# First block of a hybrid decoder layer: meta tokens loaded last and transposed in the second half, two scales earlier, weight units split in quarters

## The chip, the cores and the metric

The kernel runs on one core of one Trainium2 chip. The metric is device time in microseconds (us), as the median of several runs of the same program; smaller is better. The five engines of the core each work through a queue of their own in order: TensorE (PE; its weight loads are listed as PEld), VectorE (DVE), ScalarE (ACT), GpSimd (POOL) and SyncE (SP), which here issues the DMAs. They wait for each other through semaphores.

## The reference

One decoder layer over 16 learned meta tokens and 512 tokens of width 2048, in float32. Cut to what matters here:

```python
meta = jnp.broadcast_to(meta_tokens[None], (bsz, N_META, D_MODEL))
h_stream = jnp.concatenate([meta, x], axis=1)        # (1, 528, 2048)
hn = rmsnorm(h_stream, norm_w[l])                    # per token: x * rsqrt(mean(x*x) + eps) * w
proj = hn @ w_in[l]                                  # 2048 -> 12320 columns
c_val, c_gate, c_silu, z, xbc, dt_raw = jnp.split(proj, splits, axis=-1)
...                                                  # Conformer branch, Mamba-2 SSD branch
h_stream = h_stream + y @ w_out[l]
out = rmsnorm(h_stream, final_norm_w)[:, N_META:]
```

## The kernel before

Nearly all of the time goes to the input projection, in channel tiles of 128 columns, and to the output projection. Each product is made of three TensorE passes over operands split in a high and a low part (`hi*hi`, `hi*lo`, `lo*hi`). Both projections need the normalized tokens transposed: for each of the 16 blocks of 128 channels a tile `hnh[k]` and a tile `hnl[k]` of 128 channels x 528 tokens, the first 16 columns for the meta tokens.

The change is in the **first block**, which makes these tiles and, since tokens and weights arrive one after the other, also does the first `z` (gate) columns and the `dt` columns. It stands in a section where the order of every engine's work is written by hand, so each engine executes what the code lists, in that order:

- SP loads the meta tokens (`xm`), the token tiles `xt[0]` and `xt[1]` in halves of 512 KB, five weight units `zraw`, `xt[2]`, three more units, `xt[3]`, small parameters, and the first three weight units of the main stream (`wraw`, 512 KB each). A second copy of the meta tokens goes by GpSimd's queue, since all 128 rows of `xm` must hold finite numbers.
- TensorE first turns filler transposes (`busy`, 72 of them, constant `WARM`) until token data is there.
- The row scale of each token tile (`rs`) comes from sums of squares on ScalarE and VectorE, a square root on ScalarE (`rstd_of`) and three small VectorE steps. VectorE scales the token tiles in place (`scale`). For the meta tokens it makes `rdiag`, a diagonal matrix, so that a product of `xm` with `rdiag` scales and transposes at once.
- **First half**: for k = 0 to 15 `tok_a(k)` puts the meta product and the transposes of `xt[0]` and `xt[1]` into one PSUM bank `hta`; `fill` has ScalarE write `hnh` from it (272 columns) and queues VectorE's step for `hnl`, which `lows` hands out. Three steps later (`LAG`) `z_step` multiplies block k with its weights, six products (L357 to L359).
- **Second half**: the same for `xt[2]` and `xt[3]` (`tok_b`, bank `htb`, 256 columns), with `dt_step` for the meta tokens and `dt` columns from k = 8 on. `z_done(1)` and `z_done(2)` (k = 3 and 4) apply Silu on ScalarE, which loads another function table first. `split_unit` (k = 5, 8, 11) converts a weight unit of 1024 columns on ScalarE and subtracts on VectorE.

Four PSUM banks (`sm`) serve `hta` and `htb` in turn, so that four blocks can be on their way. A tile's readers and writers are kept apart by semaphores for the tile as a whole.

## Time and profile before

| | us |
|---|---|
| runs | 1576.78, 1576.80, 1577.02 |
| median | 1576.8 |
| the profiled execution | 1577.11 |
| its span, first to last instruction | 1575.4 |
| TensorE busy | 1565.0 (99%) |
| VectorE busy | 1070.5 (68%) |
| ScalarE busy | 536.5 (34%) |
| GpSimd busy | 51.1 (3%) |

The profiled execution is one run of the same program; its span lies 1.7 us below its time. Engine names, lines and tiles are those of the program; a row of the timeline gives the start, the duration, the engine, the line, the operation, what is written from what, how many instructions were merged (x), and in brackets how long the engine stood idle and what ended that. Matmuls overlap in the pipeline, so the time a matmul takes from a stream is the distance from its start to the next start, not its duration.

### The profile page before, as it was taken

To read this page: it belongs to the slowest core of one execution; us is meant where nothing else is said; L and a number is where in the kernel's file an instruction comes from. 1 tells how busy PE (TensorE), PEld (TensorE's weight loads), DVE (VectorE), ACT (ScalarE), POOL (GpSimd) and SP (SyncE) were. 2 spreads that over 40 slices of the span, in tenths; PEclk is the share of its full clock that TensorE was granted. 3 is DMA by queue.
4 is the path that set the end of the run, shared out by engine and by line. 5 is a ranking of instruction groups with operands and counts; after the bars stand their busy time and mean duration, and the time that the engine had idled before them with its cause. 6 is when DMAs were issued, how large, how long until landed. Compare 5 with 4: busy or idle time off the path is not lost.

```text
span 1575.4 us, 25091 instructions
## 1 busy us (share of the span) xinstructions
PE 1565.0 (99%) x10340; PEld 1437.8 (91%) x10340; DVE 1070.5 (68%) x1840; ACT 536.5 (34%) x839; POOL 51.1 (3%) x138
## 2 busy tenths in 40 slices
PE   9999999999999999999999999999999999999997
PEld 9999998999998999999899999988888888888886
DVE  7658989577998685999866899986625422232323
ACT  6443332333323333333423333324525222122313
POOL 1000000000000000000000000000000001010100
PEclk9999999999999999999999999999999999999999
DMA  8343333333333333433333333236333522222323
GB/s 225 81 114 97 102 94 100 104 92 88 110 90 102 95 106 82 108 94 99 103 97 92 99 103 92 72 108 198 94 94 108 186 95 99 99 96 94 121 94 120
DMA packets 213239, 167.27 MB, mean 106 GB/s; under 512 B 8452, under 2 KB 177252, under 8 KB 212836
## 3 DMA queue, kind: packets, MB, share of 16 engines
q1 hardware_dynamic: 212948, 165.27, 35.8%
q8 instruction: 81, 1.33, 0.4%
q14 instruction: 34, 0.28, 0.1%
q10 hardware_dynamic: 144, 0.26, 0.0%
q0 software_dynamic: 32, 0.13, 0.0%
HBM read 157.19 MB, written 8.45 MB: 105 GB/s over the span
## 4 chain that ended last, share of the span: by engine, by line
PE 99%; ACT 0%; DVE 0%; issue 0%; POOL 0%; DVEq 0%; POOLq 0%
PE o L978 8%; PE o L977 8%; PE o L979 7%; PE gt L322 4%; PE vl L322 4%; PE gt L321 4%; PE vl L321 4%; PE gt L323 4%; PE vl L323 4%; PE cs L323 4%; PE cs L321 4%; PE cs L322 4%; PE z L619 3%; PE z L618 3%; PE z L617 3%; PE xa L322 2%
## 5 line engine op out<-in xcount | busy, mean ns | idle before, releaser
L70 DVE TENSOR_TENSOR wlo<-wraw,whi 128x1024 fp32r<-128x1024 f32 x252 | 314.9, 1250 | 369.7 <-ACT whi L69 364.9
L69 ACT CAST whi<-wraw 128x1024 fp32r<-128x1024 f32 x252 | 264.4, 1049 | 738.9 <-PE o L979 246.6
L596 DVE SCALAR_TENSOR_TENSOR cv<-ub,cw,cv 128x512 f32<-128x512 f32 x480 | 359.0, 754 | 8.2
L978 PE MATMUL o<-wlo,yh 128*128 128x512 f32 x512 | 201.3, 393 | 0.0
L979 PE MATMUL o<-whi,yl 128*128 128x512 f32 x512 | 201.2, 393 | 0.0
L977 PE MATMUL o<-whi,yh 128*128 128x512 f32 x512 | 201.0, 393 | 0.0
L321 PE MATMUL vl<-hnh,whi 128*128 128x256 f32 (+1 forms) x512 | 147.0, 287 | 0.0
L321 PE MATMUL gt<-hnh,whi 128*128 128x256 f32 (+1 forms) x512 | 146.4, 286 | 0.0
L322 PE MATMUL gt<-hnl,whi 128*128 128x256 f32 (+1 forms) x512 | 146.2, 286 | 0.0
L322 PE MATMUL vl<-hnl,whi 128*128 128x256 f32 (+1 forms) x512 | 146.1, 285 | 0.0
L323 PE MATMUL gt<-hnh,wlo 128*128 128x256 f32 (+1 forms) x512 | 145.3, 284 | 0.0
L323 PE MATMUL vl<-hnh,wlo 128*128 128x256 f32 (+1 forms) x512 | 145.2, 284 | 0.0
L977 PEld LDWEIGHTS o<-whi,yh 128*128 128x128 f32 x512 | 96.2, 188 | 22.0
L978 PEld LDWEIGHTS o<-wlo,yh 128*128 128x128 f32 x512 | 96.1, 188 | 22.1
L979 PEld LDWEIGHTS o<-whi,yl 128*128 128x128 f32 x512 | 96.1, 188 | 22.1
L321 PE MATMUL cs<-hnh,whi 128*128 128x512 f32 x256 | 101.7, 397 | 0.0
L323 PE MATMUL cs<-hnh,wlo 128*128 128x512 f32 x256 | 101.0, 394 | 0.0
L322 PE MATMUL cs<-hnl,whi 128*128 128x512 f32 x256 | 100.5, 392 | 0.0
L321 PEld LDWEIGHTS gt<-hnh,whi 128*128 128x128 f32 x512 | 96.6, 189 | 0.0
L321 PEld LDWEIGHTS vl<-hnh,whi 128*128 128x128 f32 x512 | 96.5, 189 | 0.0
L323 PEld LDWEIGHTS gt<-hnh,wlo 128*128 128x128 f32 x512 | 96.5, 188 | 0.0
L323 PEld LDWEIGHTS vl<-hnh,wlo 128*128 128x128 f32 x512 | 96.5, 188 | 0.0
(891 smaller groups left out, 3455.2 us busy)
## 6 DMA issues: line engine op xcount, KB each, us to landing
wraw<-in_w_in_dram SPq DMA_DIRECT2D x188, 512.0 KB, 4.0
wraw<-in_w_out_dram SPq DMA_DIRECT2D x64, 512.0 KB, 3.6
abc<-acum_d SPq DMA_DIRECT2D x32, 256.0 KB, 3.5
yssd_d<-yout SPq DMA_DIRECT2D x16, 256.0 KB, 2.6
ysr<-yssd_d SPq DMA_DIRECT2D x16, 256.0 KB, 5.2
out_dram<-h SPq DMA_DIRECT2D x14, 256.0 KB, 2.4
xt<-in_x_dram SPq DMA_DIRECT2D x6, 512.0 KB, 7.0
h<-in_x_dram SPq DMA_DIRECT2D x3, 1024.0 KB, 7.6
```

Source lines behind the costliest of these rows:

```text
L69: nc.scalar.copy(hi[:, c], raw[:, c])
L70: engine.tensor_sub(lo[:, c], raw[:, c], hi[:, c].bitcast(F32))
L321: T.matmul(o, hi, hnh[kk][:, c0:c0 + n], start=first, stop=False)
L322: T.matmul(o, hi, hnl[kk][:, c0:c0 + n], start=False, stop=False)
L323: T.matmul(o, lo, hnh[kk][:, c0:c0 + n], start=False, stop=last)
L596: V.scalar_tensor_tensor(o, ub[:, k:k + SEQ], cw[:, KT * k + j:KT * k + j + 1], o, op0=ALU.mult, op1=ALU.add)
L617: T.matmul(o, hnh[kk][:, c0:c0 + P], hi[:, k], start=first, stop=False)
L618: T.matmul(o, hnh[kk][:, c0:c0 + P], lo[:, k], start=False, stop=False)
L619: T.matmul(o, hnl[kk][:, c0:c0 + P], hi[:, k], start=False, stop=last)
L977: T.matmul(banks[t], yhi[k][:, ts], hi[:, q], start=first, stop=False)
L978: T.matmul(banks[t], yhi[k][:, ts], lo[:, q], start=False, stop=False)
L979: T.matmul(banks[t], ylo[k][:, ts], hi[:, q], start=False, stop=last)
```

## The change

`WARM` falls from 72 to 52. The meta tokens are loaded by one DMA, after `xt[3]`; VectorE clears all of `xm` at the start; the second copy and GpSimd's two memsets of `xm` are gone. `rdiag`, the meta products (L303) and the early reduction for the meta row are gone; `tok_a` fills 256 columns. The square of the meta row moves to ScalarE at the end of the first half, its root to k = 0 of the second half, and ScalarE scales `xm` in four parts of 512 columns at k = 0 to 3. At k = 4 to 11 `tok_m` transposes two blocks of `xm` per step, four blocks to a bank `htm`, each followed by a `fill` of 16 columns. The scales of `xt[2]` and `xt[3]`, columns 512 to 1023, are handed out one token block earlier. The first three weight units are converted in quarters of 256 columns at k = 2 to 13; the loads of units 3 to 5 move accordingly. Two more filler transposes stand in the middle (14 for 12).

```diff
--- before.py
+++ after.py
@@ -37,7 +37,7 @@
 NCH = 5
 GZ = {1: 2, 3: 2, 5: 2, 7: 1}
 EARLY = 100000
-WARM = 72
+WARM = 52
 LAG = 3
 PVB = 2
 
@@ -62,12 +62,19 @@
 
     def split(self, i, raw, k, engine, parts=1):
         nc, n = self.nc, raw.shape[1]
-        hi = self.pool.tile([P, 1024], F32R, tag="whi", bufs=3, name=f"whi{i}")[:, :n]
-        lo = self.pool.tile([P, 1024], F32R, tag="wlo", bufs=3, name=f"wlo{i}")[:, :n]
+        hi, lo = self.split_tiles(i, raw)
         for q in range(parts):
             c = slice(q * n // parts, (q + 1) * n // parts)
             nc.scalar.copy(hi[:, c], raw[:, c])
             engine.tensor_sub(lo[:, c], raw[:, c], hi[:, c].bitcast(F32))
+        self.add(i, k, hi, lo)
+
+    def split_tiles(self, i, raw):
+        n = raw.shape[1]
+        return (self.pool.tile([P, 1024], F32R, tag="whi", bufs=3, name=f"whi{i}")[:, :n],
+                self.pool.tile([P, 1024], F32R, tag="wlo", bufs=3, name=f"wlo{i}")[:, :n])
+
+    def add(self, i, k, hi, lo):
         self.ready.append((hi.rearrange("p (k c) -> p k c", k=k),
                            lo.rearrange("p (k c) -> p k c", k=k)))
         self.emitted = i + 1
@@ -287,7 +294,6 @@
                 lo[:, c0:c0 + n], bank[:, :n], nw[:, k:k + 1], hi[:, c0:c0 + n].bitcast(F32),
                 op0=ALU.mult, op1=ALU.subtract))
 
-        rdiag = st.tile([P, META], F32, name="rdiag")
         later = []
 
         def lows(keep=0):
@@ -300,15 +306,14 @@
         def tok_a0(k):
             ks = slice(k * P, (k + 1) * P)
             ta[k] = sm_bank(f"hta{k}")
-            T.matmul(ta[k][:, 0:META], xm[:, ks], rdiag, start=True, stop=True)
-            T.transpose(ta[k][:, META:META + P], xt[0][:, ks], ident)
+            T.transpose(ta[k][:, 0:P], xt[0][:, ks], ident)
 
         def tok_a(k):
             ks = slice(k * P, (k + 1) * P)
             if k not in ta:
                 tok_a0(k)
-            T.transpose(ta[k][:, META + P:NA], xt[1][:, ks], ident)
-            fill(ta[k], k, 0, NA)
+            T.transpose(ta[k][:, P:2 * P], xt[1][:, ks], ident)
+            fill(ta[k], k, META, 2 * P)
 
         def tok_b(k):
             ks = slice(k * P, (k + 1) * P)
@@ -316,6 +321,16 @@
             T.transpose(b[:, 0:P], xt[2][:, ks], ident)
             T.transpose(b[:, P:2 * P], xt[3][:, ks], ident)
             fill(b, k, NA, NB)
+
+        tm = {}
+
+        def tok_m(k):
+
+            if k % 4 == 0:
+                tm[0] = sm_bank(f"htm{k}")
+            b = tm[0][:, k % 4 * P:(k % 4 + 1) * P]
+            T.transpose(b, xm[:, k * P:(k + 1) * P], ident)
+            fill(b, k, 0, META)
 
         def three(o, hi, lo, kk, c0, n, first, last):
             T.matmul(o, hi, hnh[kk][:, c0:c0 + n], start=first, stop=False)
@@ -367,7 +382,7 @@
 
         ENG = mybir.EngineType
         with tc.manual_schedule(engines={ENG.SP, ENG.Activation, ENG.DVE, ENG.Pool}):
-            nc.sync.dma_start(xm[:META], meta_tokens)
+            V.memset(xm, 0.0)
             nc.sync.dma_start(xt[0][:, :H], x[0, 0:P, :H])
             nc.sync.dma_start(xt[0][:, H:], x[0, 0:P, H:])
             nc.sync.dma_start(nwr, norm_w[0].rearrange("(j p) -> j p", p=P))
@@ -380,6 +395,7 @@
                 z_load(u)
             nc.sync.dma_start(xt[3][:, :H], x[0, 3 * P:4 * P, :H])
             nc.sync.dma_start(xt[3][:, H:], x[0, 3 * P:4 * P, H:])
+            nc.sync.dma_start(xm[:META], meta_tokens)
             nc.sync.dma_start(bias_b, dt_bias.to_broadcast([P, HEADS]))
             for r0, src in ((0, conf_dw_b), (16, conf_ln_g), (32, conf_ln_b), (48, ssd_conv_b),
                             (80, ssd_norm_w)):
@@ -392,17 +408,25 @@
             nc.sync.dma_start(a_b, A_log.to_broadcast([P, HEADS]))
             nc.sync.dma_start(dskip, D_skip.to_broadcast([P, HEADS]))
 
-            def split_unit(u):
-                stream.split(u, *units.pop(u), V)
-                units[u + 3] = stream.load(u + 3)
+            cut = {}
+
+            def split_piece(u, q):
+
+                if q == 0:
+                    if u:
+                        units[u + 2] = stream.load(u + 2)
+                    raw, kk = units.pop(u)
+                    cut[u] = (raw, *stream.split_tiles(u, raw))
+                    stream.add(u, kk, *cut[u][1:])
+                raw, hi, lo = cut[u]
+                c = slice(q * 256, (q + 1) * 256)
+                S.copy(hi[:, c], raw[:, c])
+                later.append(lambda: V.tensor_sub(lo[:, c], raw[:, c], hi[:, c].bitcast(F32)))
 
             def scales(c0, n):
                 scale(xt[0], c0, n, 1)
                 scale(xt[1], c0, n, 2)
 
-            G.dma_start(xm[META:2 * META], meta_tokens)
-            G.memset(xm[32:64], 0.0)
-            G.memset(xm[64:128], 0.0)
             for k in range(KT):
                 for h in (hnh[k], hnl[k]):
                     G.memset(h[:, 0:1].bitcast(F32), 0.0)
@@ -419,8 +443,6 @@
             busy(WARM - 8)
             T.transpose(pn[:, 0:KT], nwr, ident[:KT, :KT])
             busy(8)
-            square_dve(0, xm[:META], META)
-            quarter(0)
             square_act(1, xt[0][:, :H])
             quarter(1)
             square_act(6, xt[0][:, H:Q3])
@@ -430,8 +452,6 @@
             rstd_of(1)
             square_act(2, xt[1][:, :H])
             scale(xt[0], 0, 256, 1)
-            rstd_of(0)
-            V.tensor_scalar(rdiag, ident[:, 0:META], rs[:, 0:1], None, op0=ALU.mult)
             tok_a0(0)
             tok_a0(1)
             busy(4)
@@ -444,7 +464,7 @@
             S.copy(nw, pn[:, 0:KT])
             scale(xt[1], 0, 256, 2)
             scale(xt[0], 256, 256, 1)
-            busy(12)
+            busy(14)
             scale(xt[1], 256, 256, 2)
             z_split(0)
             lows()
@@ -460,7 +480,8 @@
                 12: lambda: (scale(xt[2], 0, 512, 3), square_act(4, xt[3][:, :H])),
                 13: lambda: (quarter(4), square_act(11, xt[3][:, H:])),
                 14: lambda: (more(4, 11), rstd_of(4)),
-                15: lambda: (scale(xt[3], 0, 256, 4), scale(xt[3], 256, 256, 4)),
+                15: lambda: (scale(xt[3], 0, 256, 4), scale(xt[3], 256, 256, 4),
+                             square_act(0, xm[:META], META)),
             }
             for k in range(KT):
                 tok_a(k)
@@ -477,6 +498,8 @@
             for k in range(KT - LAG, KT):
                 if k == KT - 1:
                     tok_b(0)
+                    scale(xt[2], 512, 512, 3)
+                    scale(xt[3], 512, 512, 4)
                 for c in (1, 2):
                     z_step(c, k)
             tok_b(1)
@@ -484,14 +507,21 @@
             tok_b(2)
             lows(1)
             zb.update({3: mm_bank("z0_3"), 4: mm_bank("z0_4"), 0: mm_bank("z0_0")})
-            scale(xt[2], 512, 512, 3)
-            scale(xt[3], 512, 512, 4)
             for k in range(KT):
                 if k + LAG < KT:
                     tok_b(k + LAG)
                     lows(1)
                 else:
                     lows()
+                if k == 0:
+                    quarter(0)
+                    rstd_of(0)
+                if k < 4:
+                    c = slice(512 * k, 512 * (k + 1))
+                    S.activation(xm[:META, c], xm[:META, c], AF.Copy, scale=rs[:META, 0:1])
+                if 4 <= k < 12:
+                    tok_m(2 * k - 8)
+                    tok_m(2 * k - 7)
                 if k == 1:
                     scale(xt[2], H, H, 3)
                 if k == 2:
@@ -503,8 +533,8 @@
                     dt_step(2 * k - 15)
                 if k in (3, 4):
                     z_done(k - 2)
-                if k in (5, 8, 11):
-                    split_unit((k - 5) // 3)
+                if 2 <= k < 14:
+                    split_piece((k - 2) // 4, (k - 2) % 4)
                 if k == 12:
                     pp = sm_bank("pp")
                     T.transpose(pp[:, 0:96], pr, ident[:96, :96])
@@ -516,6 +546,7 @@
                     for q in range(4):
                         T.transpose(pc[:, q * 124:(q + 1) * 124], cwr[:, q], ident[:124, :124])
                     V.tensor_scalar(cw, pc[:, 0:496], 0.5, None, op0=ALU.mult)
+            units[5] = stream.load(5)
             z_done(3)
             z_done(4)
             z_done(0)
```

Three places in the built program. The brackets name the semaphores that an instruction waits for (of ScalarE, VectorE, TensorE, GpSimd or a DMA queue). VectorE at the front of the block, before, from the scale of `xt[0]` (`xt_112`) to the square of `xt[1]` (`xt_113`); `ISA` is the sum of squares:

```order
L277 RECIPROCAL rs<-var 128x1 [waits DVE_49]
L280 TENSOR_SCALAR xt_112<-xt_112,rs 128x256 [waits DMAHW1_49,DVE_49]
L274 RECIPROCAL var<-root 128x1 [waits Activation_49]
L275 SCALAR_TENSOR_TENSOR var<-var,ss,root 128x1 [waits DVE_49]
L277 RECIPROCAL rs<-var 128x1 [waits DVE_49]
L434 TENSOR_SCALAR rdiag<-ident,rs 128x16 [waits DVE_49,Pool_49]
L262 TENSOR_SCALAR ss<-ss 128x1
L256 ISA junk_123,ss<-xt_113 128x512 [waits DMAHW5_49]
```

and now:

```order
L284 RECIPROCAL rs<-var 128x1 [waits DVE_49]
L287 TENSOR_SCALAR xt_112<-xt_112,rs 128x256 [waits DMAHW0_49,DVE_49]
L269 TENSOR_SCALAR ss<-ss 128x1 [waits Activation_49]
L263 ISA junk_123,ss<-xt_113 128x512 [waits DMAHW4_49]
L263 ISA ss 128x1
```

The three steps of the meta row's `rs` and `rdiag` no longer stand between them.

TensorE in the second half at k = 4, before: `htb` is the bank of `tok_b(7)`, then the six z products with `hnh[4]` and `hnl[4]`:

```order
L316 MATMUL htb_688<-ident,xt_114 128x128 [waits PE_49]
L317 MATMUL htb_688<-ident,xt_115 128x128
L357 MATMUL z_3_635<-zw_162,hnh_136 128x288 [waits Activation_49]
L358 MATMUL z_3_635<-zw_162,hnh_136 128x288
L359 MATMUL z_3_635<-zw_162,hnl_137 128x288 [waits DVE_49]
L357 MATMUL z_4_636<-zw_162,hnh_136 128x288
L358 MATMUL z_4_636<-zw_162,hnh_136 128x288
L359 MATMUL z_4_636<-zw_162,hnl_137 128x288
```

and now, up to the token transposes of k = 5 (`htm` is the bank that `tok_m` shares among four blocks):

```order
L321 MATMUL htb_659<-ident,xt_114 128x128 [waits PE_49]
L322 MATMUL htb_659<-ident,xt_115 128x128
L332 MATMUL htm_665<-ident,xm 128x128 [waits DMAHW0_49,DVE_49]
L332 MATMUL htm_665<-ident,xm 128x128 [waits Activation_49]
L372 MATMUL z_3_594<-zw_162,hnh_136 128x288
L373 MATMUL z_3_594<-zw_162,hnh_136 128x288
L374 MATMUL z_3_594<-zw_162,hnl_137 128x288
L372 MATMUL z_4_595<-zw_162,hnh_136 128x288
L373 MATMUL z_4_595<-zw_162,hnh_136 128x288
L374 MATMUL z_4_595<-zw_162,hnl_137 128x288
L321 MATMUL htb_679<-ident,xt_114 128x128 [waits DVE_49]
L322 MATMUL htb_679<-ident,xt_115 128x128
```

Two transposes of `xm` stand between the token transposes and the z products, the second one with a wait for ScalarE.

ScalarE over the same steps, before, from the fill of `tok_b(6)` to that of `tok_b(8)`:

```order
L285 ACTIVATE hnh_140<-htb_675,nw 128x256 [waits PE_49]
L346 ACT_TABLE_LOAD
L346 ACTIVATE zs_169<-z_1_390 128x256
L285 ACTIVATE hnh_142<-htb_688,nw 128x256 [waits PE_49]
L346 ACTIVATE zs_169<-z_2_391 128x256
L285 ACTIVATE hnh_144<-htb_701,nw 128x256 [waits PE_49]
```

and now, from the second scale of `xm` (L521) to the two meta fills of k = 4:

```order
L521 ACTIVATE xm<-xm,rs 16x512
L292 ACTIVATE hnh_138<-htb_627,nw 128x256 [waits PE_49]
L521 ACTIVATE xm<-xm,rs 16x512
L423 CAST whi_640<-wraw_213 128x256 [waits DMAHW1_49]
L292 ACTIVATE hnh_140<-htb_643,nw 128x256 [waits PE_49]
L521 ACTIVATE xm<-xm,rs 16x512
L361 ACT_TABLE_LOAD
L361 ACTIVATE zs_168<-z_1_360 128x256
L423 CAST whi_640<-wraw_213 128x256
L292 ACTIVATE hnh_142<-htb_659,nw 128x256 [waits PE_49]
L292 ACTIVATE hnh_128<-htm_665,nw 128x16 [waits PE_49,Pool_49]
L292 ACTIVATE hnh_130<-htm_665,nw 128x16 [waits PE_49,Pool_49]
```

The meta fills stand behind the scales of `xm`, two quarter conversions (L423), the table load with a Silu, and the fill of `tok_b(7)`; the first of the two is the one whose end the second meta transpose of TensorE waits for.

## Rows read from the trace of the kernel before

**Rows 1.** The page, chain that ended last: shares of the span by engine
```profile
PE 99%; ACT 0%; DVE 0%; issue 0%; POOL 0%; DVEq 0%; POOLq 0%
```

**Rows 2.** TensorE, whole span: line, waited for, us in total, times, longest
```profile
PE pw L417 <- POOL ident masks.py:199: 1.5, 1, 1.5
PE z L359 <- DVE hnl L286: 0.5, 1, 0.5
PE htb L316 <- DVE xt L280: 0.3, 1, 0.3
```

**Rows 3.** Timeline, front: start us, us, engine, line, operation, out<-in [idle before]
```profile
0.81 0.39 SPq L370 DMA_DIRECT2D xm<-in_meta_tokens_dram  x1
...
1.26 0.41 SPq L371 DMA_DIRECT2D xt<-in_x_dram  x1
...
1.53 9.55 PE L417 MATMUL pw<-ident 128*128 128x128 f32 x64 [1.53 <-POOL ident masks.py:199]
...
8.71 0.69 DVE L256 CUSTOM_DVE_ANT_0 junk<-xt 128x512 bf16<-128x512 f32 x1 [2.19 <-DMA xt<-in_x_dram]
...
12.02 0.23 DVE L434 TENSOR_SCALAR rdiag<-ident,rs 128x16 f32<-128x16 f32 x1
...
12.35 0.37 PE L303 MATMUL hta<-rdiag,xm 128*128 128x16 f32 x2
...
13.41 0.20 ACT L273 ACTIVATE root<-ss 128x1 f32<-128x1 f32 x1 [1.36 <-DVE ss L267]
...
14.30 0.88 DVE L280 TENSOR_SCALAR xt<-xt,rs 128x256 f32<-128x256 f32 x3
...
14.74 0.30 PE L310 MATMUL hta<-ident,xt 128*128 128x128 f32 x1
```

**Rows 4.** Timeline of TensorE, both halves of the first block
```profile
17.01 0.29 PE L303 MATMUL hta<-rdiag,xm 128*128 128x16 f32 x2
...
18.20 0.29 PE L303 MATMUL hta<-rdiag,xm 128*128 128x16 f32 x2
...
33.09 0.27 PE L316 MATMUL htb<-ident,xt 128*128 128x128 f32 x1
...
33.20 0.27 PE L317 MATMUL htb<-ident,xt 128*128 128x128 f32 x1
...
34.55 0.27 PE L316 MATMUL htb<-ident,xt 128*128 128x128 f32 x1
...
36.06 0.30 PE L316 MATMUL htb<-ident,xt 128*128 128x128 f32 x1 [0.34 <-DVE xt L280]
...
37.33 0.27 PE L316 MATMUL htb<-ident,xt 128*128 128x128 f32 x1
...
38.34 0.27 PE L316 MATMUL htb<-ident,xt 128*128 128x128 f32 x1
...
43.78 0.29 PE L358 MATMUL z<-zw,hnh 128*128 128x288 f32 x1
...
44.58 0.40 PE L359 MATMUL z<-zw,hnl 128*128 128x288 f32 x1 [0.50 <-DVE hnl L286]
```

**Rows 5.** Two stretches: length, busy PE, PEld, DVE, ACT, POOL; clock, DMA, GB/s
```profile
15.10:26.10 11.00, 11.00 (x96) 11.00 (x95) 11.00 (x25) 9.42 (x19) 0.00 (x0) 1.00 0.85 239
22.40:31.70 9.30, 9.30 (x80) 9.30 (x79) 7.82 (x23) 9.28 (x21) 0.00 (x0) 1.00 0.66 182
```

**Rows 6.** Timeline of ScalarE in the first block
```profile
13.58 0.67 ACT L338 CAST zw<-zraw 128x576 fp32r<-128x576 f32 x1
...
33.51 0.48 ACT L285 ACTIVATE hnh<-htb,nw 128x256 fp32r<-128x256 f32 x1 [1.79 <-PE htb L317]
...
34.53 1.21 ACT L285 ACTIVATE hnh<-htb,nw 128x256 fp32r<-128x256 f32 x3 [0.54 <-PE htb L317]
...
39.25 1.28 ACT L346 ACT_TABLE_LOAD   x1
...
40.83 0.47 ACT L285 ACTIVATE hnh<-htb,nw 128x256 fp32r<-128x256 f32 x1
```

## The prediction

> **What bounds the kernel now.** First the chain that ended last: TensorE holds 99% of it [rows 1]. Then TensorE's waits: over the whole span it waits three times that the profile can see, 1.5 us for the identity, 0.3 and 0.5 us in the first block, and never after 45 us [rows 2]. So TensorE's stream is the time: whatever this change does happens in the first block, before the first `xa` product, and after that a gain or loss passes through one for one. Then the timeline of the first block, engine by engine, to see who ends which wait. At the front, TensorE turns filler transposes until token data is scaled: the second half of token tile 0 lands at 8.7 us, VectorE makes `rdiag` at 12.02, the first real product starts at 12.35 and the first transpose of tile 1 at 14.74, right behind its scale at 14.30 [rows 3]. In the first half of the block a k step takes 1.19 us (17.01 to 18.20); in the second half, which has no product with `rdiag`, 1.01 us (37.33 to 38.34) [rows 4].
>
> **The change part by part.** The sum is made against the profiled execution: 1577.1 us, 1.7 us over its span; the median of the runs shown is 0.3 us lower.
>
> *Front.* Two loads of 128 KB ahead of or beside token tile 0 go, and so do `rdiag` and its reduction chain on VectorE. The issue of tile 0 moves up by 0.45 us (0.81 to 1.26) [rows 3]; with 256 KB less traffic I take 0.7 us for the landing of its second half (bounds 0.45 and 0.9, an estimate). On VectorE the two small steps and `rdiag` between the scale of tile 0 and the square of tile 1 fall away, about 0.9 us. The transpose of tile 1 thus comes at 13.1 instead of 14.74. The 18 filler transposes left take 2.0 us from 10.5 on, so they end before it; twenty fewer at the start leave a short idle time, no loss. Front: **-1.6 us** (bounds -0.9 and -2.2). The memset of `xm`, now on VectorE, lies in the empty time before 4 us.
>
> *First half.* Per k the `rdiag` product goes: 1.19 - 1.01 = 0.18 us, 16 times 2.9 us on TensorE alone. But VectorE is busy 11.00 of 11.00 us from 15.1 to 26.1, and ScalarE 9.28 of 9.30 us from 22.4 to 31.7 [rows 5], and they lose only 16 of 272 columns per block, 0.02 us. So they set the pace: some 0.5 us of slack is there up to the eighth block, 0.2 after. I take **-0.7 us** (bounds 0 and -2.5).
>
> *Scales sooner, units in quarters.* The two waits of the second half go. From 34.55 to 36.06 a step takes 1.51 instead of 1.01 us, because the scale came late; from 43.78 to 44.58 a z product, (1.01 - 0.22) / 6 = 0.13 us in the steps around, takes 0.80, because a 1024-wide conversion stood ahead of a fill [rows 4]. Sum 0.5 + 0.7 = **-1.2 us**.
>
> *Meta transposes.* Sixteen, at 0.11 us (33.09 to 33.20) [rows 4]: **+1.8 us**.
>
> *The wait that they bring.* In the built program each second meta transpose of a pair waits for ScalarE, and the value it waits for is reached by the fill that reads the first of the pair: both lie in one `htm` tile, that is in one PSUM bank. TensorE works in order, so behind that wait stand the six z products of the step and the next token transposes. And ScalarE, in order too, first has the 256-wide fill of `htb`. Counted from the second `htb` transpose: the fill starts 0.31 us later (33.20 to 33.51), takes 0.37 (three in 1.21, the last 0.48 long), the 16-wide fill up to 0.20 (a 128x1 ACTIVATE), here 0.17, the step to TensorE 0.07 [rows 3, 4, 6]. So the second meta transpose starts at 0.92 where TensorE would have it at 0.22: 0.70 us lost. The lower bound is 0.40 (nothing ahead on ScalarE), the upper 0.95. Seven of the eight pairs: 7 x 0.70 = **+4.9 us**.
>
> *The first pair, at k = 4.* Here ScalarE is far behind. From the second transpose of `htb3` (time 0) TensorE is ready for the second meta transpose after 4 x 1.01 + 0.22 = 4.3 us. ScalarE ends fill 3 at 1.0, then stands at the square root of the meta row, which waits for VectorE, and at the first scale of `xm`, 0.9 us after the root starts (13.41 to 14.30) [rows 3]: 2.2 us. Then come four 16x512 scales at 0.54 (a 128x576 CAST is 0.67 long, less with the next behind it), three fills at 0.37, two quarter conversions at 0.3, table load and Silu 1.58 (39.25 to 40.83), one fill 0.37, the meta fill and the step 0.24 [rows 6]: 2.2 + 2.2 + 1.1 + 0.6 + 1.6 + 0.4 + 0.2 = 8.3 us. Wait: 8.3 - 4.3 = **+4.0 us** (bounds 2.5 and 5). Before, the table load had the cover of three blocks of lead; the wait on ScalarE's newest fill takes that cover away.
>
> *Sum:* -1.6 - 0.7 - 1.2 + 1.8 + 4.9 + 4.0 = **+7.2 us**: 1584.3 in a profiled execution, **1584.0** as a median.
>
> A rule of the Trainium skill speaks against this part of the change: PSUM — Partial Sum Buffer, section "Summary: rules for kernel authors", tells authors to read PSUM during matmuls from another bank than the one being written, and to guard by bank. The guard is in the built program as the wait above; with one bank per transpose, as the rule has it, the +4.9 and +4.0 would fall away and the sum would be -1.7. No row of before shows a reader and a writer sharing a bank in turns.
>
> **The rivals.** *The clock falls.* TensorE would sit idle for 4 us at k = 4. The 64 filler transposes after the idle start took 9.55 us, 0.149 each, where later ones take 0.11 [rows 3, 4]: it does start slow. If it starts slow again, some three steps of 1.23 us of work take up to twice as long: +3 us, 1587. For it: the wait is longer than the 1.5 us idle at the start. Against it: it has worked without a break for 25 us by then, where at the start it came from standing still, for how long the trace does not tell. The Trainium skill, TensorE: Matmul & The Clock Gate, section "Part 1: The HAM clock gate", says that an idle TensorE is set back to the lower of its two clocks (1.2 and 2.4 GHz); by that rule this is where the extra 3 us would come from. Chance 0.15.
>
> *The waits hardly bite, and it is not slower.* Place: the eight second meta transposes. If ScalarE had always caught up and the 16-wide fill came at once, each would cost 0.40 us, 3.2 in all, and the sum would be -1.7 + 3.2 = +1.5, 1578.3: no difference to measure. It decides at 8 waits of together 4.9 us (slower by 0.2% from there on) and at 1.7 us (faster below). For it: ScalarE has idle time from 45 us on. Against it: the fill of `htb` always stands ahead, by the built order, and the table load cannot move. Chance 0.08.
>
> *The waits are not there at all*, since the chip meets them before TensorE arrives, and the first half gains its full 2.9 us: -1.7 - 2.2 = -3.9, 1572.9. Against it: a transpose and the read of its result cannot both fit into the 0.11 us between two transposes, when the read starts 0.31 after [rows 4, 6]. Chance 0.03.
>
> *The first half gives nothing*, because ScalarE and VectorE keep their own pace and token tile 3 lands no earlier: +0.7 on top, 1584.7 as a median. This lies in the range of the forecast.
>
> **How the numbers follow.** Forecast 0.74, its own range 1581 to 1587 (the six terms' bounds, not all at one end); clock 0.15; waits that hardly bite 0.08; no waits 0.03. The range 1580.5 to 1587.5 leaves out the last two and the upper part of the clock case. A measurement of this kernel tells 0.2%, 3.2 us, from no change. Slower: 0.74 + 0.15 less a little for the forecast's lower end, 0.88; same 0.09; faster 0.03.
>
> **What would show it.** Right: TensorE's waits after the change list the meta transposes waiting for the fill, eight times, 0.5 to 0.9 us each and one of about 4 us; the first transpose of token tile 1 near 13 us; the first transpose of `htb` some 2.3 us earlier than 33.1; the first `xa` product some 7 us later than before; and the two waits of before gone. Wrong in part: a first half that ends 4 us sooner (ScalarE not the bound), or no wait of 4 us at k = 4 (ScalarE caught up), which takes the sum to +3.2, the edge of what can be told. Wrong at the root: no waits for ScalarE at the meta transposes. A fallen clock shows as steps of z products more than 0.2 us apart behind the long wait.

## The result, and the profile after

| | before | changed |
|---|---|---|
| median, us | 1576.9 | 1587.1 |
| runs, us | 1576.8 to 1577.4 | 1586.2 to 1593.5 |
| profiled execution / its span, us | 1577.1 / 1575.4 | 1587.0 / 1585.3 |

By the mean of the runs the changed kernel takes 1.0071 times as long, with a 95% interval of 1.0060 to 1.0081: 11 us slower, and 10 us by the medians. The prediction had 7.2 us and ended its range at 1587.5; the median lies just inside that range, the mean of the runs, 1588.1, just outside. The direction and the place are as predicted; the sum was 3 us short.

The chain that ended last, which answers to [rows 1]: TensorE's share fell from 99% to 97%, and ScalarE, DMA and VectorE hold links in it.

```profile
PE 97%; ACT 1%; DMA 1%; DVE 1%; issue 0%; SPq 0%; DVEq 0%; ACTq 0%
```

TensorE's waits over the whole span (line, waited for, us in total, times, longest), to be set against [rows 2]. The token transpose that waited for its scale is gone, and so is the z product that waited at 44.58 [rows 4]; the 0.6 us for `hnl` in this list lie in the first half, at 30.14. New, and by far the largest, are the meta transposes (L332) that wait for ScalarE's fill (L292): eight times, as many as there are pairs, 4.4 us the longest.

```profile
PE htm L332 <- ACT hnh L292: 8.6, 8, 4.4
PE pw L441 <- POOL ident masks.py:199: 1.5, 1, 1.5
PE hta L315 <- DVE xt L287: 0.8, 1, 0.8
PE z L374 <- DVE hnl L293: 0.6, 1, 0.6
PE z L372 <- ACT hnh L292: 0.6, 1, 0.6
```

TensorE's timeline: the first transpose of token tile 1 (L315), the first token transpose of the second half (L321), then the first three pairs of meta transposes (L332) with two z products behind the first, the odd ones of the next two pairs, and the first `xa` product. In each pair the first transpose is called even here, the second, which waits, odd. The first odd one starts 4.63 us after its even one, the next two 0.94 and 0.90 after theirs.

```profile
12.27 0.33 PE L315 MATMUL hta<-ident,xt 128*128 128x128 f32 x1 [0.79 <-DVE xt L287]
...
30.77 0.27 PE L321 MATMUL htb<-ident,xt 128*128 128x128 f32 x1
...
36.51 0.27 PE L332 MATMUL htm<-ident,xm 128*128 128x128 f32 x1
41.14 0.48 PE L332 MATMUL htm<-ident,xm 128*128 128x128 f32 x1 [4.36 <-ACT hnh L292]
...
41.65 0.44 PE L373 MATMUL z<-zw,hnh 128*128 128x288 f32 x1
41.89 0.44 PE L374 MATMUL z<-zw,hnl 128*128 128x288 f32 x1
...
43.27 0.42 PE L332 MATMUL htm<-ident,xm 128*128 128x128 f32 x1
44.21 0.48 PE L332 MATMUL htm<-ident,xm 128*128 128x128 f32 x1 [0.52 <-ACT hnh L292]
...
46.07 0.27 PE L332 MATMUL htm<-ident,xm 128*128 128x128 f32 x1
46.97 0.33 PE L332 MATMUL htm<-ident,xm 128*128 128x128 f32 x1 [0.62 <-ACT hnh L292]
...
49.03 0.33 PE L332 MATMUL htm<-ident,xm 128*128 128x128 f32 x1 [0.58 <-ACT hnh L292]
...
51.11 0.33 PE L332 MATMUL htm<-ident,xm 128*128 128x128 f32 x1 [0.62 <-ACT hnh L292]
...
63.55 0.37 PE L336 MATMUL xa<-hnh,whi 128*128 128x272 f32 x1
```

ScalarE's timeline shows what stood ahead of that first meta fill (40.81): an idle time for the meta row's scale, the four scales of `xm` (L521, three of them here), the table load, a Silu and the fill of `htb` (40.44). ScalarE has no idle time between 34.63 and 41.09.

```profile
34.63 0.72 ACT L521 ACTIVATE xm<-xm,rs 16x512 f32<-16x512 f32 x1 [0.69 <-DVE rs L284]
...
36.59 0.70 ACT L521 ACTIVATE xm<-xm,rs 16x512 f32<-16x512 f32 x1
...
37.86 0.70 ACT L521 ACTIVATE xm<-xm,rs 16x512 f32<-16x512 f32 x1
38.57 1.28 ACT L361 ACT_TABLE_LOAD   x1
39.87 0.38 ACT L361 ACTIVATE zs<-z 128x256 f32<-128x256 f32 x1
40.15 0.40 ACT L423 CAST whi<-wraw 128x256 fp32r<-128x256 f32 x1
40.44 0.48 ACT L292 ACTIVATE hnh<-htb,nw 128x256 fp32r<-128x256 f32 x1
40.81 0.28 ACT L292 ACTIVATE hnh<-htm,nw 128x16 fp32r<-128x16 f32 x1
```

The stretches around it (length, busy PE, PEld, DVE, ACT, POOL; then granted clock, DMA share, GB/s). TensorE does nothing from 36.8 to 41.1, and in that time the granted clock goes to 0.50, that is from 2.4 to 1.2 GHz; it is back at 1.00 after 46.

```profile
38.00:40.00 2.00, 0.00 (x0) 0.00 (x0) 0.04 (x1) 1.98 (x3) 0.00 (x0) 0.73 0.13 28
40.00:42.00 2.00, 0.86 (x4) 0.86 (x5) 0.91 (x3) 1.37 (x6) 0.00 (x0) 0.50 0.00 0
42.00:44.00 2.00, 1.69 (x8) 1.24 (x6) 1.19 (x5) 1.03 (x4) 0.00 (x0) 0.50 0.00 0
44.00:46.00 2.00, 1.79 (x9) 1.79 (x10) 1.20 (x4) 0.73 (x3) 0.00 (x0) 0.56 0.00 0
46.00:48.00 2.00, 1.38 (x12) 1.14 (x10) 0.79 (x4) 1.21 (x4) 0.00 (x0) 1.00 0.32 79
```

The first `xa` product comes at 63.55 us; before, at 53.54:

```profile
53.54 0.37 PE L321 MATMUL xa<-hnh,whi 128*128 128x272 f32 x1
```

So all 10 us of the profiled execution arise ahead of it, as the prediction had it.

### The profile page after: what moved, and what is told of

Read it like the earlier page. It is cut to its first block, busy times and chain, and to the rows that moved or that the text cites. A ratio compares the mean times of both kernels' runs of the same rounds, so it can differ in the third digit from the quotient of the medians.

```text
span 1585.3 us, 25058 instructions
## 1 busy us (share of the span) xinstructions
PE 1565.3 (99%) x10306; PEld 1435.6 (91%) x10306; DVE 1073.4 (68%) x1863; ACT 545.2 (34%) x870; POOL 46.8 (3%) x135
## 4 chain that ended last, share of the span: by engine, by line
PE 97%; ACT 1%; DMA 1%; DVE 1%; issue 0%; SPq 0%; DVEq 0%; ACTq 0%
PE o L1009 7%; PE o L1008 7%; PE o L1010 7%; PE gt L337 4%; PE vl L337 4%; PE gt L336 4%; PE vl L336 4%; PE gt L338 4%; PE vl L338 4%; PE cs L338 4%; PE cs L336 4%; PE cs L337 4%; PE z L650 3%; PE z L649 3%; PE z L648 3%; PE xa L337 2%
## 5 line engine op out<-in xcount | busy, mean ns | idle before, releaser
L69 DVE TENSOR_TENSOR wlo<-wraw,whi 128x1024 fp32r<-128x1024 f32 x249 | 311.2, 1250 | 367.4 <-ACT whi L68 362.6
```

Source lines behind the costliest of these rows:

```text
L69: engine.tensor_sub(lo[:, c], raw[:, c], hi[:, c].bitcast(F32))
```

## The experiments

The theory: the loss is TensorE's waits for ScalarE, because transposes and their readers take turns on one bank, first behind a backlog on ScalarE and then at every pair, and the idle TensorE loses its clock on top. Rivals: the turns are not the cause but ScalarE is the bound in any form; the later load itself is to blame; the clock has no share in it. The ratios and intervals below are against runs of before on the same chip (medians 1576.7 to 1577.1). The edits are cut to the lines that matter.

**Both transposes of a pair ahead of both fills.** One turn fewer per pair.

```diff
-                    tok_m(2 * k - 8)
-                    tok_m(2 * k - 7)
+                    tok_m(2 * k - 8, 2)   # two transposes, then two fills
```

> The changed kernel, but both meta transposes of a step stand ahead of their two fills, so that none waits for ScalarE to read the one before. Theory (bank turns, behind a ScalarE that is late): the second pair of each bank (k = 5, 7, 9, 11) still waits for the reads of the first pair in it. At k = 5 that is the same late ScalarE, some 4 us; at k = 7, 9, 11 about 0.3 us each. The other waits go (4 x 0.6 and the 4.4 moves by one step): total about 1580 to 1582, the lower end if the clock does not fall. Rival (only the order inside a pair costs, ScalarE's lateness does not): all eight waits go, about 1575.

Measured 1582.1 (1.0032 times before, 1.0020 to 1.0043): 5.0 us off the changed kernel. Its waits:

```profile
PE htm L333 <- DVE hnl L293: 4.6, 1, 4.6
```

The eight waits for ScalarE have become one, and that one is the second pair's, which writes into the bank that the first pair's readers still hold (VectorE's `hnl` steps, which follow ScalarE's fills). This order is rid of the short turns, not of the backlog. The granted clock fell here too, to 0.50 from 42 to 46 us.

**Four transposes per bank ahead of their four fills**, at k = 4, 6, 8 and 10: a bank is written once.

```diff
-                if 4 <= k < 12:
-                    tok_m(2 * k - 8)
-                    tok_m(2 * k - 7)
+                if 4 <= k < 12 and k % 2 == 0:
+                    tok_m(2 * k - 8, 4)
```

> The changed kernel with four meta transposes at k = 4, 6, 8 and 10, each group in a bank of its own, ahead of its four fills: no bank is written again while ScalarE still has to read it for the same group. Theory: no wait for a meta fill is left; what is left of ScalarE's lateness shows at k = 6, where the next bank in the turn is that of the token block whose fill stands behind the table load, some 2 us; the clock does not fall. Total about 1577, near the kernel before. Rival (TensorE loses the time to something else, the meta transposes only show it): still above 1583.

Measured 1579.8 (1.0019, 1.0009 to 1.0028): another 2.4 us, but 2.8 above what was expected. Two waits for banks remain, and the granted clock fell here too, which the theory had ruled out, with no wait of TensorE longer than 2.0 us. VectorE's timeline has the reason for the first wait: its addition for dt, in order ahead of the low halves that free the banks, stood 2.24 us until ScalarE had done the Silu on the same bank.

```profile
PE htb L321 <- DVE hnl L293: 2.0, 1, 2.0
PE htm L333 <- DVE hnl L293: 1.2, 1, 1.2
```

```profile
40.79 0.19 DVE L364 TENSOR_TENSOR dts<-z,bias_b 128x32 f32<-128x32 f32 x1 [2.24 <-ACT zs L363]
40.90 0.47 DVE L293 SCALAR_TENSOR_TENSOR hnl<-htb,nw,hnh 128x256 fp32r<-128x256 f32 x1
```

```profile
40.00:42.00 2.00, 0.44 (x2) 0.20 (x2) 0.91 (x3) 1.99 (x9) 0.00 (x0) 1.00 0.00 0
42.00:44.00 2.00, 0.97 (x5) 0.97 (x6) 1.61 (x8) 1.70 (x6) 0.00 (x0) 0.71 0.00 0
44.00:46.00 2.00, 2.00 (x10) 1.98 (x10) 1.95 (x8) 1.06 (x5) 0.00 (x0) 0.50 0.09 16
```

**Filler transposes in the long wait**, so that TensorE is not idle.

```diff
+            if k == 0:
+                for _ in range(38):
+                    T.transpose(tm[0][:, 3 * P:], ident, ident)
```

> The changed kernel with 38 filler transposes of the identity (4.1 us) ahead of the first meta transpose, in the stretch where TensorE stands idle for 4.4 us. Theory (the idle time lets the clock fall to 1.2 GHz, and the two steps after it cost 1.7 us more than the later ones): the first wait shrinks to under 1 us, the first second-of-pair transpose starts at about the same time (41.1 to 41.3), the z products after it stand 0.13 us apart instead of 0.24, total 1585.4, and the runs spread less. Rival (the products are slow for another reason, as ScalarE's reads or the weights): z products at 0.24 as before, total 1587 or more.

Measured 1586.2 (1.0060, 1.0043 to 1.0077), the profiled execution 1585.4, 1.6 us under that of the changed kernel. The granted clock stays at 1.00 through the stretch:

```profile
40.00:42.00 2.00, 1.50 (x11) 1.11 (x9) 0.84 (x4) 1.30 (x6) 0.00 (x0) 1.00 0.00 0
42.00:44.00 2.00, 1.07 (x7) 0.88 (x8) 1.18 (x5) 1.02 (x4) 0.00 (x0) 1.00 0.00 0
```

The 1.6 us are not the clock's alone, though. From the first `htb` transpose to the first `xa` product it took 31.95 us (29.99 to 61.94), in the changed kernel 32.78 (30.77 to 63.55): 0.83 less. The rest is the first half, where ScalarE did not have to wait for token tile 3 this time (17.64 us against 18.50). That the forecast of 1585.4 was met is in part luck. What the fall costs is read from the changed kernel's own steps: from one odd meta transpose to the next it took 3.07 and 2.76 us while the clock was down, 2.06 and 2.08 after it (rows above), so 1.7 us in all. With the fillers the z products there stand 0.13 us apart instead of 0.24, so the slow steps are gone; but the first odd transpose came 0.2 us later than in the changed kernel, counted from the first `htb` one, and the second pair met a new wait of 0.6 us:

```profile
PE htm L335 <- DVE hnl L293: 0.6, 1, 0.6
```

The turns stand without the fall: eight waits for ScalarE, 4.5 us in all. Two of the four runs took 1586.9 and 1587.5 at a lower mean clock (0.998 and 0.997, the others 0.999); it may have fallen in those in spite of the fillers, but only the profiled execution has a trace.

**The four scales of `xm` on VectorE**, to take them out of ScalarE's backlog.

```diff
-                    S.activation(xm[:META, c], xm[:META, c], AF.Copy, scale=rs[:META, 0:1])
+                    scale(xm, 512 * k, 512, 0, META)
```

> The changed kernel with the four scales of the meta rows on VectorE instead of ScalarE. Theory (ScalarE's work ahead of the first meta fill makes the long wait): four times 0.63 us and a wait of 0.7 us for the root's chain leave ScalarE's queue ahead of that fill; the first wait falls from 4.4 to about 2 us, the other seven stay at 0.5 to 0.6; with an idle time of 2 us the clock stays up: 1587.1 - 2.4 - 1.7 = 1583.0. If the clock falls after 2 us too: 1584.7. Rival (the table load alone makes the wait): the first wait stays above 3.5 us, total 1586 to 1587.

Profiled 1583.9, 0.9 us over what was expected; the median of four runs 1586.0 (1.0062, 1.0042 to 1.0083). The profiled execution kept its clock, with a mean of 0.999; the other three, at 0.992 to 0.996, took 1585.7 to 1592.0. The longest wait fell from 4.4 to 1.5 us, by more than the four scales' 2.5 (34.63 to 38.57 above, less the work in between), because ScalarE no longer stood 0.69 us for the meta row's scale either and went straight on to the next fill.

```profile
PE htm L332 <- ACT hnh L292: 5.6, 8, 1.5
PE htm L332 <- DVE hnl L293: 1.0, 2, 0.6
```

**The two Silus later**, with the table load, in the changed kernel. This takes another summand out of the same backlog.

```diff
-                if k in (3, 4):
-                    z_done(k - 2)
+                if k in (5, 7):
+                    z_done(k // 2 - 1)
```

> The changed kernel with nothing else but its two Silus, and the table load ahead of the first, at k = 5 and 7 instead of 3 and 4. In the changed kernel they stood in the backlog ahead of the first meta fill, from 38.57 to 40.15 us. Theory: ScalarE's backlog is a plain sum, so the wait of 4.36 us at the first odd transpose falls by these 1.6 us to about 2.8, and comes back at the pair of k = 6, whose fill now stands behind the table load: TensorE's waits for ScalarE are as large in sum (8.6 us), and the time is 1587, less up to 1.7 us where the granted clock does not fall. Rival: the backlog is set by the scales' waits for VectorE, and the table load lay beside them: first wait still above 4 us.

```profile
PE htm L332 <- ACT hnh L292: 7.9, 8, 2.7
```

The first wait fell by 1.7 us to 2.7, and 1.1 of it came back at the pair of k = 6, whose wait went from 0.6 to 1.7: the sum of the eight only went from 8.6 to 7.9. The profiled execution took 1585.5; the median of four runs, 1588.8 (1585.5 to 1592.6), tells no difference from the changed kernel. So in these two runs ScalarE's backlog behaves as a plain sum, and where a fill stands behind it TensorE pays.

**The scales sooner and the quarters alone**, in the kernel before.

```diff
+                    scale(xt[2], 512, 512, 3)      # after tok_b(0), not after tok_b(2)
+                    scale(xt[3], 512, 512, 4)
...
-                if k in (5, 8, 11):
-                    split_unit((k - 5) // 3)
+                if 2 <= k < 14:
+                    split_piece((k - 2) // 4, (k - 2) % 4)
```

> The kernel before with one part of the change alone: the two scales handed out sooner and the first three weight units split in quarters; the meta tokens stay where they were. Theory: this part gains about what the prediction gave it, 1.2 us, since tok_b(3) to tok_b(7) took 4.82 us before and 4.07 in the changed kernel, and whole splits of 0.9 us stood ahead of fills further on: 1575.7 us. Rival: the quarters only cut one piece of work into four with their own fixed cost, and the gap is taken up by the next wait: 1576.9, no difference.

Measured 1575.35 (0.9989, 0.9980 to 0.9999), 1.5 us under before. The theory holds. This is the part of the change that pays by itself; the later load, with the second copy gone, gains 2.5 us at the front and gives back far more in the second half. Of all waits of [rows 2] only that at the start is left:

```profile
PE pw L435 <- POOL ident masks.py:199: 1.5, 1, 1.5
```

**Four per bank and the scales on VectorE** together.

> The changed kernel with four transposes per bank ahead of their four fills, and the four scales of xm on VectorE instead of ScalarE. With four per bank alone, VectorE stood 2.24 us at its dt addition for ScalarE's Silu, and TensorE then waited 2.0 and 1.2 us for banks that VectorE had to give back. Theory: ScalarE was late by the four scales of 0.63 us; without them the Silu comes about 2.5 us sooner, both waits go, and with them the fall of the granted clock: 1577 us. Rival: the four scales now hold VectorE for 1.9 us in the same stretch, and the banks come back as late: 1580, as with four per bank alone.

Measured 1576.5 (0.9997, 0.9988 to 1.0006), as the theory had it. The wait of 2.0 us is gone, the clock stays at 1.00, and the two waits left come to 1.5 us:

```profile
PE htm L333 <- DVE hnl L293: 1.5, 2, 1.2
```

**The same, with scales and groups two steps later**, past the Silus.

```diff
-                if k < 4:
-                    scale(xm, 512 * k, 512, 0, META)
-                if 4 <= k < 12 and k % 2 == 0:
-                    tok_m(2 * k - 8, 4)
+                if 2 <= k < 6:
+                    scale(xm, 512 * (k - 2), 512, 0, META)
+                if 6 <= k < 14 and k % 2 == 0:
+                    tok_m(2 * k - 12, 4)
```

> As four per bank with the scales on VectorE, but the scales and the groups of transposes two steps later (groups at k = 6, 8, 10, 12, the last still two steps ahead of its dt product). There TensorE waited 0.33, 0.23, 0.38 and 1.17 us for VectorE's lows, in the stretch where ScalarE had the table load of 1.28 us and two Silus to do. Theory: the stretch is short of time only until the Silus are done, at 39.9 us; two steps later the same groups cost their 1.8 us of transposes and no wait: 1576.5 - 2 = 1574.5 us. Rival: the waits come from the fifth bank user in the rotation of four, wherever it stands: 1576.5, the same. Second rival: the dt products then wait for their lows: 1577.5.

Measured 1575.8 (0.9993, 0.9984 to 1.0002), profiled 1574.9. The median lies between the theory and the rival; the trace decides for the theory, since the groups' waits fell from 1.5 to 0.3 us:

```profile
PE htm L333 <- DVE hnl L293: 0.3, 1, 0.3
```

**The Silus later instead**, groups as they were.

> As four per bank with the scales on VectorE, but the two Silus (with the table load ahead of the first) stand at k = 5 and 7 instead of 3 and 4; the groups stay at k = 4, 6, 8, 10. Theory: the table load and the Silu hold ScalarE, and VectorE's dt addition behind the Silu holds the lows; with both later the waits of 0.33 to 1.17 us at the first two groups go, and smaller ones come further on: 1575 us. Rival: the bank that z0_0 takes over comes free later and the first dt product waits for the second Silu: 1576.5 to 1577.5.

Measured 1576.1 (0.9995, 0.9986 to 1.0004); the groups' waits 0.6 us in two. Between these three kernels the medians differ by less than their spread, but the traces point one way: what held the groups was ScalarE's work in that stretch, not a fifth user of four banks, since each of the two moves away from it cut the groups' waits. The first `xa` product came at 53.15, 51.46 and 52.31 us.

**A product with a diagonal in the second half**, eight into one bank, instead of scales and transposes.

```diff
-            b = tm[0][:, k % 4 * P:(k % 4 + 1) * P]
-            T.transpose(b, xm[:, k * P:(k + 1) * P], ident)
+            for j in range(8):
+                T.matmul(tm[0][:, j], xm[:, (k + j) * P:(k + j + 1) * P], rdiag,
+                         start=True, stop=True)
```

> The changed kernel, its meta tokens still loaded last, but scaled and transposed in the second half by a product with a diagonal of 16 columns as the kernel before did, eight products side by side in one bank at k = 4 and eight at k = 8, their fills spread over three steps each; no scaling of xm on ScalarE, no turns between TensorE and ScalarE on one bank. Theory: the loss of the changed kernel is the turns and ScalarE's lateness, and nothing in the later load itself: the front's 2.3 us and the quarters' 1.2 us come out, the 16 products cost the second half about 1 us: 1574.4 us. Rival: VectorE's dt addition waits for the Silu behind the table load and gives the banks back late, as with four transposes per bank: 1576.5. Second rival: the work in the second half is bound by ScalarE whatever its form: 1579 or more.

Measured 1579.0 (1.0014, 1.0005 to 1.0023), 4.6 us over what was expected. The second rival has the number, but not the cause: TensorE's list has no wait for ScalarE. Its timeline shows that the eight products (sixteen records) hold it for 1.74 us, from 36.31 to the next z product at 38.05, 0.22 each, where a transpose takes 0.11. TensorE's weight loads are sixteen for the eight products too, two for each, where a transpose has one. Both groups cost 3.6 us and not 1.

```profile
36.31 1.89 PE L331 MATMUL htm<-rdiag,xm 128*128 128x16 f32 x16
```

The other 2 us are the clock, which fell from 46 to 50 us, and a new wait of 0.8 us for a bank. Two steps there took 1.96 and 1.92 us (46.24 to 48.20 to 50.12), where one takes 1.18 (46.50 to 47.68 in the kernel before), so the fall cost about 1.5 us. The next kernel, with the same products, no such fall and no such wait, took 1577.2.

**The same, and token tile 3 loaded ahead of z units 6 and 7.**

> As the kernel with the late products, and the last token tile xt[3] is loaded ahead of the z weights of units 6 and 7. ScalarE stood 0.81 us for that tile in the changed kernel, and the first half took 18.50 us where the prediction had 17.65. Theory: the landing of xt[3] set the end of the first half; 0.6 us sooner than with the late products alone. Rival: ScalarE catches up before tok_b(0) anyway: no difference. Second rival: units 6 and 7 now land after TensorE wants them: slower by up to 1 us.

Measured 1577.2 (1.0001, 0.9993 to 1.0010). The theory falls: the first half took 18.62 us in its profile and 17.64 without the move. Without it ScalarE did not have to wait for the tile in that execution; with it ScalarE waited for a z unit that was put behind. The median is lower than without the move for another reason, the clock and the bank wait just named.

```profile
24.69 0.67 ACT L352 CAST zw<-zraw 128x576 fp32r<-128x576 f32 x1 [0.86 <-DMA zraw<-in_w_in_dram]
```

**The meta tokens first in the queue again**, all else as changed.

```diff
+            nc.sync.dma_start(xm[:META], meta_tokens)
             nc.sync.dma_start(xt[0][:, :H], x[0, 0:P, :H])
...
-            nc.sync.dma_start(xm[:META], meta_tokens)
             nc.sync.dma_start(bias_b, dt_bias.to_broadcast([P, HEADS]))
```

> The changed kernel with one line moved back: the meta tokens are the first transfer of the queue again (once, without the second copy that the kernel before made from GpSimd's queue); they are still scaled and transposed in the second half. In the kernel before, the second half of tile 0 was there at 8.7 us, in the changed one at 5.9, and TensorE reached the first transpose of tile 1 at 12.27 instead of 14.74, 2.5 us sooner where the prediction had 1.6. Theory: the place in the queue did this; with the meta tokens first the second half of tile 0 lands near 8.7 us again, the first transpose of tile 1 comes near 14, and the whole takes some 1.5 us more, 1588.6 us. Rival: the gain came from VectorE's square of the meta tokens and its products, or from the second copy, which are still gone: tile 1 near 12.7, and 1587.

Measured 1589.8 (1.0084, 1.0070 to 1.0098), 2.7 us over the changed kernel. The first transpose of tile 1 came at 15.50 in place of 12.27, 3.2 us later, which seems to bear the theory out. But the edit changes more than a place in the queue: VectorE clears all of `xm` first, and a load into `xm` that stands behind the clearing has to wait for it. SP works in order, so all its loads waited too; the first started at 3.09 us, where the changed kernel's first starts at 0.80.

```profile
1.30 1.76 DVE L385 MEMSET xm<- 128x2048 f32 x1 [1.30 <-PEq L1081]
...
3.09 0.39 SPq L386 DMA_DIRECT2D xm<-in_meta_tokens_dram  x1
```

```profile
15.50 0.33 PE L315 MATMUL hta<-ident,xt 128*128 128x128 f32 x1 [1.70 <-DVE xt L287]
```

Of the 3.2 us, 2.3 are this wait, which leaves some 0.9 for the place in the queue, 0.45 of it the issue. How long tile 0's second half was under way says the same. Before, VectorE could start on it 7.0 us after its issue (1.72 to 8.71) and had waited for nothing else; in the changed kernel, 4.6 us after it (1.25 to 5.85); here, with the meta tokens at the head of the queue, 4.9 at most (3.99 to 8.92, and VectorE had waited for ScalarE). So the head of the queue does not bring the slow transfer of before back, and the theory is not borne out. Of the rival, VectorE's square is no cause either, since VectorE had waited 2.19 us for the transfer [rows 3]. The second copy of the meta tokens, which GpSimd's queue issued at 1.98 in the kernel before, is left; no run leaves out that copy alone, so the cause stays open.

## Why the prediction was right in kind and short in size

The mechanism stands: the second transpose of a pair waits for the fill of the first, eight times, and the front gains. The step that failed is the clock, which the sum had at nothing and which cost 1.7 us; beside it the turns and the first pair were sized 1.5 us too small, and a front that gained 0.9 us more than forecast hid part of this. By terms (us; "before" and "changed" are the two profiled executions):

| term | predicted | measured | from |
|---|---|---|---|
| front | -1.6 | -2.5 | tile 1 at 12.27, was 14.74 [rows 3] |
| first half | -0.7 | +0.15 | 18.50 (12.27 to 30.77), was 18.35 (14.74 to 33.09) [rows 3, 4] |
| scales, quarters | -1.2 | -1.5 | run alone |
| meta transposes | +1.8 | +1.8 | 0.11 each in the kernel with later groups |
| first pair | +4.0 | +4.5 | 41.14 where 36.62 was due |
| seven turns | +4.9 | +5.9 | odd to odd 2.07, due 1.23 |
| clock | 0 | +1.7 | odd to odd 3.07 and 2.76, then 2.07; z products 0.24 apart from 41.6 to 45.5 |
| sum | +7.2 | +10.0 | first `xa` product 63.55, was 53.54 |

*Front: mis-sized, and its two parts are wrong.* The second half of tile 0 could be read 2.9 us sooner (5.85, before 8.71 [rows 3]), not 0.7, the estimate made from bytes; what made this transfer slow before is open, as the run with the meta tokens first shows. The 0.9 us for VectorE's small steps did not come: from that square to the scale of tile 1 it took 6.0 us (5.85 to 11.86), before 5.6 (8.71 to 14.30), since ScalarE, which had tile 1's first half at hand before, now waited for it:

```profile
5.85 0.69 DVE L263 CUSTOM_DVE_ANT_0 junk<-xt 128x512 bf16<-128x512 f32 x1
```

```profile
8.54 1.06 ACT L260 ACTIVATE junk<-xt 128x1024 bf16<-128x1024 f32 x1 [1.29 <-DMA xt<-in_x_dram]
```

The runs with the late load put the first transpose of tile 1 between 12.27 and 12.94. That the first `htb` transpose came 2.3 us earlier, just as forecast, is luck: the front gave 0.9 us more and the first half 0.85 less than their terms.

*First half: right, but for a transfer that came late.* VectorE and ScalarE are the pace, and the products that left are worth little, as the text had it. From the first transpose of tile 1 to the first of `htb` it took 18.35 us before and 17.63 or 17.64 in the profiles of seven of the kernels run, 0.7 less to the digit; in an eighth 17.47. In the profile of the changed kernel, and in three more (18.14 to 18.62), ScalarE waited 0.5 to 0.9 us for a transfer on top, for token tile 3 in all but the kernel that moved it. Here:

```profile
25.47 1.06 ACT L260 ACTIVATE junk<-xt 128x1024 bf16<-128x1024 f32 x1 [0.81 <-DMA xt<-in_x_dram]
```

That the first half might give nothing was in the text as a case inside the range, and tile 3 was named in it; what the runs add is that it depends on the execution.

*Scales and quarters: right*, 0.3 us small.

*Meta transposes: borne out.* In the kernel with four per bank and later groups a step with a group and no wait in it takes 1.61 us (43.55 to 45.16), the step ahead of it, without a group, 1.17 (42.38 to 43.55): 0.44 for four transposes, 0.11 each. The whole second half up to `xa` takes 21.5 us there, 2.6 more than with the quarters alone (18.9): 1.8 for the transposes, 0.3 for the wait shown, and some 0.5 in small gaps that are not traced.

*The turn: right in kind, 0.14 us too small each.* The 16-wide fill takes 0.28 us (40.81 above), and the prediction took 0.17 from a 128x1 operation, the shortest row that it had; the upper bound of 0.20 was below the truth. Of the 0.84 us of a turn the wait list shows 0.5 to 0.6; most of the rest is lost overlap, since a transpose lasts 0.27 us and the next would start 0.11 after its start.

*The first pair: right in kind, 0.5 us small.* The scales of `xm` took 0.63 us each, not 0.54. The two runs that took a summand out of the backlog moved the wait by about what they took: 2.9 us for the scales and the wait ahead of them, which measured 3.2, and 1.7 for table load and Silu, which measured 1.6.

*The clock: the step that failed.* It was a rival with a chance of 0.15, for lack of a row that tells how TensorE fares after a long idle time in mid-work. It came in the profiled execution, where TensorE was idle from 36.8 to 41.1 us and was granted 0.50 from 40 to 44 at the least; in the other runs the mean clock, 0.990 to 0.997 against 0.998 and 0.999 before, points to the same. Its price was 1.7 us, under the 3 that the rival gave. The Trainium skill, TensorE: Matmul & The Clock Gate, section "Part 1: The HAM clock gate", says that an idle TensorE is set back to the lower clock; the trace agrees, and the chance should have followed it. With the rival's price of 3 us the forecast would have been 1587.0.

The rule of the same skill that the prediction weighed, PSUM — Partial Sum Buffer, section "Summary: rules for kernel authors" (read from another bank than the one being written), fits the runs with four transposes per bank, where the next group goes to another bank than the one being read: with ScalarE's backlog out of the way they come to -0.3, -1.1 and -0.8 us against before. The -1.7 that the prediction worked out for a bank per transpose was not reached; VectorE's waits of 0.3 to 1.5 us were not in it.

Of the kernels run, the quarters alone, without the meta part, is the fastest: 1.5 us under before and almost 12 under the changed kernel. Four per bank with later groups is level with it within the spread.

## What to carry to other kernels

Before a step is moved under an engine that works in order, write down who reads its result, from which bank, and what that reader has queued ahead at that moment: a backlog that cost nothing behind three blocks of lead is paid in full by the first step that waits for the newest result. Write all of a bank's transposes before the first of their reads; it costs the same instructions. Where a forecast puts TensorE idle for microseconds, price the clock into the forecast, not into a rival. And when an experiment moves one line back, read the start of the engine that it touches before the total: here the moved load brought a wait of its own, and the total alone would have borne out the wrong theory.

## What the runs showed of the hardware that was not expected

- The granted clock fell with no wait longer than 2.0 us. With four per bank TensorE was busy 0.44 of 2 us and then 0.97 of 2, and was granted 0.50 when it was fully busy again (the rows above). With fillers it was busy 1.07 to 1.50 of 2 and kept 1.00.
- Kernels with turns spread, and the time goes with the mean clock of the run: the changed kernel took 1586.2 us at 0.997 and 1593.5 at 0.990, with the Silus later 1585.5 at 0.997 and 1592.6 at 0.991; the runs of before that stand beside the experiments lie within 1.7 us, all at 0.998 or 0.999. In which stretch the longest runs lost their clock isn't known, since only the profiled execution has a trace.
- A product of 16 columns took 0.22 us in a row of eight, with two 128x128 weight loads each; a 128x128 transpose, with one, took 0.11.
- The same code took 17.5 to 18.5 us in the first half, as a transfer landed in time or not: before a microsecond of difference between two profiles of this block is put down to a change elsewhere, that wait has to be taken off.
- A transfer of 512 KB was ready for use 7.0 us after its issue in the kernel before, and 4.6 and at most 4.9 us after it in the two kernels without the second copy of the meta tokens, whether or not the meta tokens stood ahead of it in the queue.
